# Norms between the branches of a two-layer decoder step: unread matmuls in TensorE's wait, the residual updated by VectorE alone in pairs of tiles, the next norm's squares moved into the following group

## Chip, cores and metric

One Trainium2 chip, and on it one core. The metric is the device time of one execution in microseconds (us), the median over the runs shown. The profile is of one execution, recorded by the hardware profiler.

## What is computed

A step of a hybrid decoder with two layers, for 256 prompt tokens and 32 sample tokens (288 columns in all, D = 2048 features). Each layer is a mixer branch and a feed-forward branch, each between two RMS norms, with a residual `h` that lives through the whole step:

```python
for l in range(DEPTH):                      # DEPTH = 2
    a = _rms(h, norm_mix_pre[l])
    y = mixer(a)                            # even layer: pooling and retention; odd layer: spatial gating and convolution (width 31)
    h = h + _rms(y, norm_mix_post[l])
    f = _rms(h, norm_ffn_pre[l])
    f = square(relu(f @ w_up[l])) @ w_down[l]
    h = h + _rms(f, norm_ffn_post[l])

def _rms(x, g):
    return x * rsqrt(mean(x * x, axis=-1) + EPS) * g
```

All in float32. Where one branch ends and the next begins, the kernel must thus finish a norm of `y`, add it to `h`, and start the norm of `h`. There are four such ends; the change touches the three that lie between branches (the last has code of its own).

## The kernel before

Features lie on the 128 partitions and tokens in the 288 columns, so `h` is 16 tiles `[128, 288]` in one buffer. Weights stream from HBM in pieces of 128x1024 floats. Each piece is split in two so that the faster float32r matmul gives full precision: ScalarE writes the rounded part `whi` (`emit_hi`), VectorE the rest `wlo = raw - whi` (`emit_lo`); activations are split in the same way into `xhi` (ScalarE, `make_hi`) and `xlo` (VectorE, `make_lo`). One piece is called a sub. `emit_mm` issues its 24 matmuls (line 522): two row blocks by four output blocks by three products (hi·hi, lo·hi, hi·lo). Subs are collected in groups of eight (four in the odd layer's output projection), each with 512 outputs in four banks of PSUM; five banks exist, and a bank comes free when its evacuation has read it.

The order on each engine is the order in which `run()` emits. For each sub it emits some `whi` (a ring of three to five subs), one step of a `pre` generator if the group has one, the `wlo`s, the matmuls, and then `bg_step()`, which advances each background generator in `bgs` by one `yield`. A second list, `fills`, holds work that is emitted only while a small meter per engine says there is room; the odd layer's convolution is there: `conv_all` (five of eight channel tiles, 31 taps each on VectorE, the rows `conv<-gx` and `odds<-gx`) and `conv_pool` (three tiles, taps on ScalarE with adds on GpSimd). They start when the first odd group has been evacuated, and `post_o` drains what is left of them behind the first half of the output projection, followed by `conv_out`, the convolution's layer norm.

A boundary is the `pre` generator of the first group of a branch (`boundary`, line 344). `last_rs()` sums the squares of `y` with matmuls of one column (line 273); GpSimd takes the power -0.5 (`sm`); `spread` broadcasts the result over the partitions with six float32 passes (line 252) into a bank `pb`. Then, for each tile k: `grow_h` (VectorE: `tmp = y * pb`), `add_h` (`h += tmp`; VectorE for tiles 0, 1 and the even ones, GpSimd for the odd ones), `make_hi`, the square of `h` on ScalarE with its add into `accs[1]` on GpSimd (`add_sq`), and, one pair later, `make_lo`. The first group uses `xhi` and `xlo` without the pre-norm's factor, as that is a factor per token: its results are copied to `y` tiles (`defer`), and a background generator `rest` runs `finish_pre` (sums the squares, spreads the factor, copies it to `rb`) and then evacuates the group with `rb`. Later groups are evacuated with `rb` directly.

Of the kernel before, what the change touches and what calls it, by code (L numbers as in the profile page):

```python
# [19 lines left out]
T = SEQ + NS  # L20
# [83 lines left out]
class Meter:  # L104
    """an engine, with the work that is emitted on it and, by estimate, not done yet"""

# [27 lines left out]
def build(tc, ctx, I, O, C):  # L134
# [12 lines left out]
    def tmp():  # L147
        return tp.tile([128, T], F32, tag="tmp", name="tmp")
# [10 lines left out]

    # ------------------------------------------------------------ loads  # L160
    xth = [cp.tile([128, 2, D // 2], F32, tag=f"hidhi{i}", name="xth") for i in range(2)]
# [65 lines left out]

    # ------------------------------------------------------------ norms
    P = {}
# [9 lines left out]
    def rs_from(cols, d):  # L239
        """cols: the sums of 128 or fewer tokens each"""  # L240
        sm = next_small()
        for t, c in enumerate(cols):
            V.tensor_scalar(out=sm[:c.shape[0], t:t + c.shape[1]], in0=c, scalar1=1.0 / d, scalar2=EPS, op0=MUL,
                            op1=ADD)
        G.tensor_tensor(out=sm[:, 4:7], in0=sm[:, 0:3], in1=mhalf[:, 0:3], op=ALU.pow)
        return sm[:, 4:7]
# [9 lines left out]
    def sum_open(rep=None):  # L256
        """the tokens' sums over the features of parts to come; with rep the sample's four times over"""
        P["sums"] = [bank(), 0, rep]
# [81 lines left out]
    def y(k):  # L340
        return Y[k // 8][:, k % 8, :]

    # ------------------------------------------------------------ boundaries
    def boundary(layer, which):
        post = (1, 3)[which]
        nxt = (2, layer) if which == 0 else (0, layer + 1)
        rs = last_rs()
        pb = spread(rs)
        new_x()

        def grow_h(k):
            t = tmp()
            V.tensor_tensor(out=t, in0=y(k), in1=pb[:, :T], op=MUL)
            return t

        def add_h(k, t, eng):
            eng.tensor_tensor(out=h[:, k, :], in0=h[:, k, :], in1=t, op=ADD)

        def first(k):
            make_hi(k, gain(nxt[0], nxt[1], k))  # L360
            add_sq(accs[1], k, h[:, k, :])

        def second(k):
            make_lo(k, gain(nxt[0], nxt[1], k))

        for k in (0, 1):
            add_h(k, grow_h(k), V)
            first(k)
        second(0)
        second(1)  # L370
        for a in range(2, KT, 2):
            tb = grow_h(a + 1)
            add_h(a + 1, tb, G)
            ta = grow_h(a)
            if a > 2:
                second(a - 2)
                second(a - 1)
            add_h(a, ta, V)
            first(a)
            first(a + 1)  # L380
            yield
        second(KT - 2)
        second(KT - 1)
        yield
        yield
# [4 lines left out]
    def last_tiles(src, m):  # L390
        """the squares of the last tiles go to the row sums by themselves"""
        if m < OWN:
            add_sq(accs[0], 12 + m, src)
            return
        s = tmp()
        A.activation(out=s, in_=src, func=AF.Square)
        P["own", m] = s
# [7 lines left out]
    def last_rs():  # L405
        sum_part(accs[0])
        for m in range(OWN, 4):
            sum_part(P["own", m])
        return sum_rs(D)

    def finish_pre():
        yield
        ps = var_of(accs[1])
        yield
        rs = rs_from(ps, D)
        yield
        pb = spread(rs)
        A.copy(out=rb, in_=pb[:, :T])
        yield

    # ------------------------------------------------------------ background work
    bgs, fills = [], []
# [16 lines left out]

    # ------------------------------------------------------------ the stream of weights  # L440
    groups = []
# [49 lines left out]
    def feed_hi(to):  # L491
        """the weights' first parts up to sub to, and more weights on their way"""
        while W["split"] <= min(to, len(subs) - 1):
            fetch()
            emit_hi(W["split"])
            W["split"] += 1
# [7 lines left out]
    def some(n):  # L504
        """n subs more, as far as the ring goes beyond the sub at hand"""
        return min(W["split"] + n - 1, W["now"] + RING + W["extra"] - 1)
# [121 lines left out]

    # ------------------------------------------------------------ feed-forward
    def ffn(layer, last):  # L630
# [56 lines left out]

    # ------------------------------------------------------------ even layer
    evo, ne = _cols(C_EVEN)
# [128 lines left out]
    def ret_k(j):  # L818
        """what the two heads' queries and keys give alone"""
        ep, qk = E["pool"], E["qk"]  # L820
# [72 lines left out]
    def piece(R, j, p):  # L893
        """two batches of a head's sample group: their rows' part from the old state, and the new state"""
        hh, b = p // 4, 2 * (p % 4)
# [175 lines left out]

    # ------------------------------------------------------------ odd layer
    odo, no = _cols(C_ODD)
# [93 lines left out]
    def conv_slow(ct):  # L1167
        """one channel tile's taps on the scalar and Pool engines"""
        dw = dwT.rearrange("p (k t) -> p t k", t=8)
        gx, acc = Q["gx"][ct], Q["conv"][:, ct, 0:SEQ]  # L1170
        for k in range(CK):
            while not room(((A, CAPA), (G, CAPG))):
                yield
            w = dw[:, ct, k:k + 1]
            if k == 0:
                A.activation(out=acc, in_=gx[:, 0:SEQ], func=AF.Identity, scale=w, bias=vec("dw_b", ct))
            else:
                t = Q["pool"].tile([128, SEQ], F32, tag="tap", name="tap", bufs=4)
                A.activation(out=t, in_=gx[:, k:k + SEQ], func=AF.Copy, scale=w)
                G.tensor_tensor(out=acc, in0=acc, in1=t, op=ADD)  # L1180
# [69 lines left out]
    def layer_norm(src, n):  # L1250
        """src(k): tiles [128, T], their sum in accs[1]; centres them in place and leaves the factor in Q"""
        yield
# [227 lines left out]

    # ------------------------------------------------------------ first layer's input
    def prologue():
# [45 lines left out]

    # ------------------------------------------------------------ the end
    F = {}  # L1530

    def end_h():
        """the residual turned token-major while the last feed-forward runs"""
        F["h"] = W["pool"].tile([128, 2, D], F32, tag="hT", name="hT", bufs=1)
        F["hs"] = W["pool"].tile([128, 512], F32, tag="hTs", name="hTs", bufs=1)
        for k in range(KT):
            turn_tile(h[:, k, :], F["h"], F["hs"], k, A)
            yield
# [74 lines left out]
```

## Time and profile before

| what | value |
|---|---|
| median of 3 runs | 2537.54 us (2537.18 to 2537.67) |
| span of the profiled execution | 2536.2 us |
| TensorE busy | 2436.1 us (96%) |
| VectorE busy | 1397.9 us (55%) |
| ScalarE busy | 1120.8 us (44%) |
| GpSimd busy | 384.4 us (15%) |
| mean granted TensorE clock | 0.981 |
| the three boundaries, first `y * pb` on VectorE | at 456.0, 1286.0 and 1683.9 us |

The page names no time of the profiled execution other than its span from the first to the last instruction; the runs' median lies 1.3 us above it. In the profile PE is TensorE, DVE VectorE, ACT ScalarE and POOL GpSimd. A helper records most instructions of DVE, ACT and POOL, so that they all carry line 119; they are told apart by the names of their tiles, output first. The granted clock is a share of 2.4 GHz: 1.00 is 2.4 GHz, 0.50 is 1.2 GHz, and a value between is a stretch with some of each.

### The profile page before, as it was taken

The numbers are of one execution on the slowest core, as the hardware profiler recorded it, in microseconds if no ns is written. First come the engines' busy times: TensorE is split into PE (matmuls) and PEld (weight loads), VectorE is DVE, ScalarE is ACT, GpSimd is POOL, SyncE is SP. The second block draws the span as 40 slices with busy tenths as digits, with TensorE's granted clock in tenths as the row PEclk, the third lists the DMA queues.
The fourth block names the chain that finished last, engine by engine and source line by source line (L and its number), as shares of the span: only waits on it lengthen the run. The fifth ranks groups of instructions, "written<-read, shape, count | busy, mean of one in ns | idle before, by whom it ended". The sixth has DMA issues, their size and how long they took to land.

```text
span 2536.2 us, 43599 instructions
## 1 busy us (share of the span) xinstructions
PE 2436.1 (96%) x18060; PEld 2400.4 (95%) x18060; DVE 1397.9 (55%) x1838; ACT 1120.8 (44%) x1648; POOL 384.4 (15%) x440
## 2 busy tenths in 40 slices
PE   7999999899999999999988889789999999999998
PEld 6989999899999999999988889789999999999997
DVE  5555564754354445454478978665434444544454
ACT  4443433553443344344454555555444433433453
POOL 2321121300000000000137764340000000000010
PEclk9999999899999999999999999889999999999999
DMA  6556555455555555555444435336555555555542
GB/s 192 165 172 194 171 176 173 133 167 167 166 167 166 166 166 167 167 166 167 158 136 137 131 117 160 112 112 180 169 157 166 166 167 166 165 167 166 167 158 96
DMA packets 220612, 403.52 MB, mean 159 GB/s; under 512 B 14593, under 2 KB 44077, under 8 KB 220358
## 3 DMA queue, kind: packets, MB, share of 16 engines
q1 hardware_dynamic: 214446, 383.53, 49.4%
q0 software_dynamic: 5440, 16.75, 2.1%
q8 instruction: 141, 2.31, 0.4%
q10 hardware_dynamic: 528, 0.46, 0.1%
q14 instruction: 57, 0.47, 0.1%
HBM read 390.77 MB, written 10.95 MB: 158 GB/s over the span
## 4 chain that ended last, share of the span: by engine, by line
PE 84%; DVE 9%; issue 3%; ACT 2%; POOL 1%; DMA 0%; DVEq 0%; POOLq 0%; ACTq 0%
PE mm L522 80%; DVE wlo L119 3%; DVE conv L119 2%; DVE odds L119 1%; DVE tmp L119 1%; DVE xlo L119 1%; DVE h L119 1%; ACT tmp L119 1%; ACT whi L119 1%; PE ms L904 1%; POOL acc L119 0%; PE ms L908 0%; PE ms L1543 0%; PE ms L273 0%; PE ms L252 0%
## 5 line engine op out<-in xcount | busy, mean ns | idle before, releaser
L119 DVE TENSOR_TENSOR wlo<-raw,whi 128x1024 fp32r<-128x1024 f32 x720 | 893.3, 1246 | 808.7 <-ACT whi L119 808.2
L119 ACT ACTIVATE whi<-raw 128x1024 fp32r<-128x1024 f32 x720 | 759.5, 1059 | 1030.3 <-PE mm L522 982.8
L522 PE MATMUL mm<-xhi,whi 128*128 128x288 f32 x3200 | 954.4, 299 | 32.8 <-DVE tmp L119 27.1
L522 PE MATMUL mm<-xhi,wlo 128*128 128x288 f32 x3200 | 953.0, 299 | 18.9 <-DVE wlo L119 18.8
L522 PE MATMUL mm<-xlo,whi 128*128 128x288 f32 x3200 | 924.8, 298 | 0.0
L522 PE MATMUL mm<-hidhi,whi 128*128 128x288 f32 x2560 | 752.0, 295 | 3.5 <-ACT hidhi L119 3.5
L522 PE MATMUL mm<-hidhi,wlo 128*128 128x288 f32 x2560 | 753.9, 295 | 0.9 <-DVE wlo L119 0.9
L522 PE MATMUL mm<-hidlo,whi 128*128 128x288 f32 x2560 | 742.5, 295 | 0.0
L522 PEld LDWEIGHTS mm<-xhi,whi 128*128 128x128 f32 x3200 | 612.9, 192 | 35.7 <-DVE tmp L119 28.5
L522 PEld LDWEIGHTS mm<-xhi,wlo 128*128 128x128 f32 x3200 | 612.5, 191 | 23.7 <-DVE wlo L119 23.4
L522 PEld LDWEIGHTS mm<-xlo,whi 128*128 128x128 f32 x3200 | 601.4, 191 | 0.0
L522 PEld LDWEIGHTS mm<-hidhi,whi 128*128 128x128 f32 x2560 | 482.2, 188 | 4.1 <-ACT hidhi L119 3.6
L522 PEld LDWEIGHTS mm<-hidhi,wlo 128*128 128x128 f32 x2560 | 482.2, 188 | 1.1 <-DVE wlo L119 1.1
L522 PEld LDWEIGHTS mm<-hidlo,whi 128*128 128x128 f32 x2560 | 477.4, 188 | 0.0
L119 POOL TENSOR_TENSOR acc<-acc,tmp 128x288 f32<-128x288 f32 x107 | 102.7, 960 | 1720.6 <-ACT tmp L119 1715.5
L119 POOL TENSOR_TENSOR conv<-conv,tap 128x256 f32<-128x256 f32 x90 | 89.6, 996 | 57.9 <-ACT tap L119 52.8
L119 DVE SCALAR_TENSOR_TENSOR u<-mm,rb 128x288 f32<-128x288 f32 x120 | 54.9, 457 | 78.8 <-PE mm L522 78.8
L119 DVE TENSOR_TENSOR y<-mm,y 128x288 f32<-128x288 f32 x112 | 51.0, 457 | 84.4 <-PE mm L522 84.4
L119 ACT ACTIVATE xhi<-h,gT 128x288 fp32r<-128x288 f32 x64 | 33.8, 529 | 64.1 <-DVE h L119 64.1
L119 ACT ACTIVATE u<-u 128x288 f32<-128x288 f32 x128 | 55.3, 432 | 10.0 <-DVE u L119 10.0
L119 ACT ACTIVATE hidhi<-u 128x288 fp32r<-128x288 f32 x128 | 56.9, 445 | 4.1
L119 DVE SCALAR_TENSOR_TENSOR conv<-gx,dwT,conv 128x256 f32<-128x256 f32 x75 | 54.5, 726 | 0.0
(237 smaller groups left out, 1090.3 us busy)
## 6 DMA issues: line engine op xcount, KB each, us to landing
raw<-in_w_up SPq DMA_DIRECT2D x256, 512.0 KB, 3.8
raw<-in_w_down SPq DMA_DIRECT2D x256, 512.0 KB, 3.8
raw<-in_w_in_even SPq DMA_DIRECT2D x56, 512.0 KB, 3.7
raw<-in_w_out_even SPq DMA_DIRECT2D x32, 512.0 KB, 4.0
raw<-in_w_in_odd SPq DMA_DIRECT2D x64, 256.0 KB, 3.0
raw<-in_w_in_odd SPq DMA_DIRECT2D x32, 512.0 KB, 3.7
raw<-in_w_out_odd SPq DMA_DIRECT2D x32, 512.0 KB, 4.3
raw<-in_w_in_even SPq DMA_DIRECT2D x48, 256.0 KB, 3.5
```

Source lines behind the costliest of these rows:

```text
L119: return call(*args, **kw)
L522: PE.matmul(ps, lhsT=lhsT[:, k, c], rhs=rhs, start=s == 0 and k == 0 and which == 0, stop=last and k == 1 and which == 2)
L904: PE.matmul(po[gq:gq + 32, 0:256], lhsT=E["qdm"][:, hh, 32 * (b + i):32 * (b + i + 1)], rhs=s[:, i, :], start=False, stop=b >= 4, tile_pos ...
```

## The change

Three things at each of the three boundaries.

1. `keep_warm(n)` issues n float32 matmuls of 128x288 into a bank that nothing reads: two behind the one-column sums, three behind `spread`.
2. The residual is updated by VectorE alone, in place in the `y` tiles, and from tile 2 on two tiles (576 columns) in one instruction; `tmp` buffers and GpSimd are no longer used for it.
3. The squares of `h` and their adds leave the boundary. `finish_pre` issues them, four tiles a step, so they stand in the group behind the boundary's first one, and everything that waits for `rb` (the evacuation of the first group, and what that starts) comes four subs later.

```diff
+    def keep_warm(n):
+        ps = bank()
+        for _ in range(n):
+            PE.matmul(ps[:, :T], lhsT=ones, rhs=accs[0][:, :T], start=True, stop=True)
+
     def boundary(layer, which):
-        post = (1, 3)[which]
         nxt = (2, layer) if which == 0 else (0, layer + 1)
         rs = last_rs()
+        keep_warm(2)
         pb = spread(rs)
+        keep_warm(3)
         new_x()
 
-        def grow_h(k):
-            t = tmp()
-            V.tensor_tensor(out=t, in0=y(k), in1=pb[:, :T], op=MUL)
-            return t
-
-        def add_h(k, t, eng):
-            eng.tensor_tensor(out=h[:, k, :], in0=h[:, k, :], in1=t, op=ADD)
-
-        def first(k):
-            make_hi(k, gain(nxt[0], nxt[1], k))
-            add_sq(accs[1], k, h[:, k, :])
+        def grow(k, n):
+            t = Y[k // 8][:, k % 8:k % 8 + n, :]
+            V.tensor_tensor(out=t, in0=t, in1=pb[:, :T].unsqueeze(1).to_broadcast([128, n, T]), op=MUL)
+            V.tensor_tensor(out=h[:, k:k + n, :], in0=h[:, k:k + n, :], in1=t, op=ADD)
+            for i in range(n):
+                make_hi(k + i, gain(nxt[0], nxt[1], k + i))
 
         def second(k):
             make_lo(k, gain(nxt[0], nxt[1], k))
 
-        for k in (0, 1):
-            add_h(k, grow_h(k), V)
-            first(k)
+        grow(0, 1)
+        grow(1, 1)
         second(0)
         second(1)
         for a in range(2, KT, 2):
-            tb = grow_h(a + 1)
-            add_h(a + 1, tb, G)
-            ta = grow_h(a)
+            grow(a, 2)
             if a > 2:
                 second(a - 2)
                 second(a - 1)
-            add_h(a, ta, V)
-            first(a)
-            first(a + 1)
             yield
...
     def finish_pre():
+        for a in range(0, KT, 4):
+            for k in range(a, a + 4):
+                add_sq(accs[1], k, h[:, k, :])
+            yield
         yield
         ps = var_of(accs[1])
```

How the order moves, at the three places of which the prediction speaks.

VectorE at the first boundary: tiles 6 and 7, the `wlo` of the group's third sub, tiles 8 and 9, the next `wlo`. Before (`ms` is the bank `pb`, `y_3861` and `y_3862` are the two halves of `y`):

```order
L119 TENSOR_TENSOR tmp<-y_3861,ms 128x288 x2
L119 SCALAR_TENSOR_TENSOR xlo<-h,gT,xhi 128x288 x2
L119 TENSOR_TENSOR h<-h,tmp 128x288
L119 TENSOR_TENSOR wlo<-raw,whi 128x1024
L119 TENSOR_TENSOR tmp<-y_3862,ms 128x288 x2
L119 SCALAR_TENSOR_TENSOR xlo<-h,gT,xhi 128x288 x2
L119 TENSOR_TENSOR h<-h,tmp 128x288
L119 TENSOR_TENSOR wlo<-raw,whi 128x1024
```

Now:

```order
L119 TENSOR_TENSOR y_3861<-y_3861,ms 128x576
L119 TENSOR_TENSOR h<-h,y_3861 128x576
L119 SCALAR_TENSOR_TENSOR xlo<-h,gT,xhi 128x288 x2
L119 TENSOR_TENSOR wlo<-raw,whi 128x1024
L119 TENSOR_TENSOR y_3862<-y_3862,ms 128x576
L119 TENSOR_TENSOR h<-h,y_3862 128x576
L119 SCALAR_TENSOR_TENSOR xlo<-h,gT,xhi 128x288 x2
L119 TENSOR_TENSOR wlo<-raw,whi 128x1024
```

Per pair of tiles VectorE has one product and one add of 576 columns where it had two products and one add of 288; the other add was GpSimd's. The `wlo`s keep their places between the pairs.

ScalarE at the end of the first boundary's group. Before:

```order
L119 ACTIVATE xhi<-h,gT 128x288
L119 ACTIVATE tmp<-h 128x288
L119 ACTIVATE whi<-raw 128x1024 x2
L119 COPY y_3861<-mm 128x288 x4
L119 ACTIVATE whi<-raw 128x1024 x6
L119 COPY rb<-ms 128x288
```

Now (`acc_76` is `accs[1]`, `tmp<-h` a square):

```order
L119 COPY y_3861<-mm 128x288 x4
L119 ACTIVATE acc_76<-h 128x288
L119 ACTIVATE tmp<-h 128x288 x3
L119 ACTIVATE whi<-raw 128x1024 x2
L119 ACTIVATE tmp<-h 128x288 x4
L119 ACTIVATE whi<-raw 128x1024 x2
L119 ACTIVATE tmp<-h 128x288 x4
L119 ACTIVATE whi<-raw 128x1024 x2
L119 ACTIVATE tmp<-h 128x288 x4
L119 ACTIVATE whi<-raw 128x1024 x4
L119 COPY rb<-ms 128x288
```

Four squares now stand between the copies of the first group and the `whi` of the next group's second sub, and four more behind each two `whi`.

VectorE in the odd layer, where the first half of the output projection ends and `conv_out` begins (the last `wlo`, the end of the taps, the first instruction of the layer norm). Before:

```order
L119 SCALAR_TENSOR_TENSOR odds<-gx,dwT,odds 128x256
L119 TENSOR_TENSOR wlo<-raw,whi 128x1024
L119 SCALAR_TENSOR_TENSOR conv<-gx,dwT,conv 128x256
L119 TENSOR_TENSOR conv<-conv,odds 128x256
L119 TENSOR_TENSOR wlo<-raw,whi 128x1024
L119 TENSOR_TENSOR conv<-conv,mean 128x288 x8
```

Now, the end of the same stretch; between its `wlo` and the `wlo` ahead of that stand seven taps, and behind it eleven, of which the last six are shown:

```order
L119 SCALAR_TENSOR_TENSOR odds<-gx,dwT,odds 128x256
L119 SCALAR_TENSOR_TENSOR conv<-gx,dwT,conv 128x256
L119 SCALAR_TENSOR_TENSOR odds<-gx,dwT,odds 128x256
L119 SCALAR_TENSOR_TENSOR conv<-gx,dwT,conv 128x256
L119 SCALAR_TENSOR_TENSOR odds<-gx,dwT,odds 128x256
L119 SCALAR_TENSOR_TENSOR conv<-gx,dwT,conv 128x256
L119 TENSOR_TENSOR conv<-conv,odds 128x256
L119 TENSOR_TENSOR conv<-conv,mean 128x288 x8
```

Of the 155 taps one stood behind the last `wlo` but one; now 18 do.

## Rows read from the trace of the kernel before

**Rows 1.** The page, part 1: busy time, share of the span, instructions.

```profile
PE 2436.1 (96%) x18060; PEld 2400.4 (95%) x18060; DVE 1397.9 (55%) x1838; ACT 1120.8 (44%) x1648; POOL 384.4 (15%) x440
```

**Rows 2.** TensorE's waits, whole span: total us, times, longest us.

```profile
PE mm L522 <- DVE tmp L119: 27.1, 6, 9.1
PE mm L522 <- DVE wlo L119: 19.6, 18, 2.8
```

**Rows 3.** Timeline of TensorE, first boundary: start us, us, instruction, [idle before <-releaser].

```profile
450.82 2.13 PE L273 MATMUL ms<-cg,tmp 128*128 128x1 f32 x18
454.41 1.49 PE L252 MATMUL ms<-cg,sm 128*128 128x128 f32 x6 [1.46 <-POOL sm L119]
457.57 0.61 PE L522 MATMUL mm<-xhi,whi 128*128 128x288 f32 x1 [1.67 <-ACT xhi L119]
...
469.11 0.40 PE L522 MATMUL mm<-xhi,wlo 128*128 128x288 f32 x1 [2.07 <-DVE wlo L119]
```

**Rows 4.** Windows of 1 us there: busy PE, PEld, DVE, ACT, POOL, PEclk, DMA, GB/s.

```profile
453.00:454.00 1.00, 0.00 (x0) 0.00 (x0) 0.38 (x3) 0.00 (x0) 0.50 (x1) 0.71 0.35 57
...
457.00:458.00 1.00, 0.43 (x2) 0.43 (x3) 0.97 (x3) 1.00 (x3) 0.00 (x0) 0.50 0.04 8
...
463.00:464.00 1.00, 1.00 (x7) 1.00 (x7) 1.00 (x2) 0.17 (x1) 1.00 (x2) 0.67 0.00 0
```

**Rows 5.** Timeline of VectorE, first boundary.

```profile
456.00 0.46 DVE L119 TENSOR_TENSOR tmp<-y,ms 128x288 f32<-128x288 f32 x1 [2.59 <-PE ms L252]
...
458.85 0.81 DVE L119 TENSOR_TENSOR tmp<-y,ms 128x288 f32<-128x288 f32 x2
...
467.85 1.21 DVE L119 TENSOR_TENSOR wlo<-raw,whi 128x1024 fp32r<-128x1024 f32 x1
468.98 0.81 DVE L119 TENSOR_TENSOR tmp<-y,ms 128x288 f32<-128x288 f32 x2
469.71 1.49 DVE L119 SCALAR_TENSOR_TENSOR xlo<-h,gT,xhi 128x288 fp32r<-128x288 f32 x2
471.12 1.05 DVE L119 TENSOR_TENSOR h<-h,tmp 128x288 f32<-128x288 f32 x1
472.10 1.21 DVE L119 TENSOR_TENSOR wlo<-raw,whi 128x1024 fp32r<-128x1024 f32 x1
```

**Rows 6.** VectorE by form: a product with PSUM, 512 columns: busy us, mean ns.

```profile
L119 DVE TENSOR_TENSOR smk<-ms,ce 128x512 f32<-128x512 f32 x3 | 2.1, 685 | 0.9 <-PE ms L845 0.9
```

**Rows 7.** Timeline of TensorE: one float32 matmul of 128x288, two passes.

```profile
76.22 0.65 PE L779 MATMUL ms<-tmp,wpl 128*128 128x288 f32 x2
```

**Rows 8.** Timeline of ScalarE: end of the first boundary's group; later, three squares.

```profile
492.69 0.40 ACT L119 COPY y<-mm 128x288 f32<-128x288 f32 x1 [0.39 <-PE mm L522]
492.98 3.90 ACT L119 ACTIVATE whi<-raw 128x1024 fp32r<-128x1024 f32 x4
...
1610.13 1.18 ACT L119 ACTIVATE tmp<-conv 128x288 f32<-128x288 f32 x3
```

**Rows 9.** Timeline of GpSimd: adds of squares; the sums ahead of the layer norm.

```profile
481.74 1.93 POOL L119 TENSOR_TENSOR acc<-acc,tmp 128x288 f32<-128x288 f32 x2 [1.36 <-ACT tmp L119]
...
1590.46 6.42 POOL L119 TENSOR_TENSOR acc<-acc,conv 128x288 f32<-128x288 f32 x6
```

**Rows 10.** Timeline of VectorE, odd layer: a deferred evacuation, a tap beside GpSimd, taps alone.

```profile
1337.67 1.19 DVE L119 TENSOR_TENSOR tmp<-y,rb 128x288 f32<-128x288 f32 x3
...
1382.48 1.05 DVE L119 SCALAR_TENSOR_TENSOR conv<-gx,dwT,conv 128x256 f32<-128x256 f32 x1
...
1602.49 0.47 DVE L119 SCALAR_TENSOR_TENSOR conv<-gx,dwT,conv 128x256 f32<-128x256 f32 x1
1602.88 0.47 DVE L119 SCALAR_TENSOR_TENSOR odds<-gx,dwT,odds 128x256 f32<-128x256 f32 x1
```

**Rows 11.** Timeline of TensorE, odd layer: behind the third group, and the drain.

```profile
1389.71 0.61 PE L522 MATMUL mm<-xhi,whi 128*128 128x288 f32 x1 [9.14 <-DVE tmp L119]
...
1607.97 0.75 PE L1255 MATMUL ms<-acc,cg 128*128 128x288 f32 x2 [1.54 <-POOL acc L119]
```

## The prediction, made before the change was run

> **What bounds the kernel now.** The page's first part says that TensorE is busy in 96% of the span [rows 1], so only the remaining 100 us, or work taken from TensorE itself, can be won. The change adds a little TensorE work and moves none of it, so I read which waits stand at the boundaries. In TensorE's waits, those for VectorE's `wlo` sum to 19.6 us and those for its `tmp` to 27.1 us [rows 2]. The timeline of the first boundary shows where they lie: behind the one-column sums TensorE waits 1.46 us for GpSimd's power, runs the six passes of `spread`, waits 1.67 us for the first `xhi`, and later 2.07 us for the third sub's `wlo` [rows 3]. The windows show that the clock has already dropped when `spread` runs: 0.71, then 0.50 in the first sub, and up again at 463 to 464 [rows 4].
>
> The cause of the `wlo` waits is VectorE's own pace. One period of the first group (`wlo`, two products, two `xlo`, one add) runs from 467.85 to 472.10, that is 4.25 us [rows 5]. A mean matmul is 2436.1 us / 18,060 = 0.135 us [rows 1], so 24 of them are 3.2 us: inside this group TensorE is fed more slowly than it could work. VectorE, then, sets the end of that group.
>
> **Residual on VectorE, in pairs.** VectorE takes over GpSimd's add, but pays less per column. One product of 512 columns with PSUM takes 0.685 us [rows 6], so 576 columns are about 0.76, or 0.80 with the step to the add that needs it. Two products of 288 take 0.81 [rows 5]; an add of 576 columns is one instruction for two, so I take 0.66, between 0.5 and 0.81. The adds of 288 that now take 1.05 us and the two `xlo` that take 1.49 are that slow while GpSimd works on `h` beside them: a tap, which like `xlo` has two inputs and a factor, takes 1.05 us beside GpSimd and alone comes every 0.39 us for 256 columns [rows 10]. With GpSimd silent I take 0.42 for each `xlo`. A `wlo` is 1.13 to the next start [rows 5]. So a period is 0.80 + 0.66 + 0.84 + 1.13 = 3.43 us in place of 4.25, still above TensorE's 3.2. The third sub's `wlo` now starts 11.85 us after the first product [rows 5]. The opening two single tiles keep their 2.85 us (456.00 to 458.85); three pairs (1.46 each with their dependence) and four `xlo` of 0.42 follow, 8.9 us in all: 2.9 earlier. Four more periods give 4 x 0.82 = 3.3. The group's end comes 6.2 us earlier at each of three boundaries, bounds 4 (sharing goes on) and 7.
>
> **Unread matmuls.** One float32 matmul of 288 columns is two passes in 0.65 us from first start to last end [rows 7], of which some 0.48 is passes; at the half clock double. Two fit into the 1.46 us wait at full clock and overrun it by up to 0.5 us at half; three take 1.44 or 2.9 us against the 1.67 us wait [rows 3] and can hold back the first sub by up to 1.2. That is covered: sub three waits for VectorE, not for TensorE, and the group ends when VectorE ends. If that cover were gone it would cost the same 1.2 us. I book nothing, with ends of -0.75 and +0.5 at each boundary.
>
> Does the clock stay up? In the rows, TensorE records are busy from 450.82 to 452.95 with one-column matmuls and the clock falls just behind them; it comes back six microseconds after the dense products begin at 457.57 [rows 3, 4]. Being "busy" with thin matmuls did not hold it. I take it that 1.4 us of dense matmuls between two gaps does not reliably do so either. The Trainium skill ("TensorE: Matmul & The Clock Gate", section "What's actually happening") says that the throttled clock is the default and that activity releases it; by that rule dense matmuls in the gap could keep it released, which is a rival below, while the trace shows a fall behind records that count as busy.
>
> **Squares later.** They leave ScalarE's and GpSimd's work in the first group, where they cost TensorE nothing, and enter the next one. Three squares take 1.18 us, so four take 1.57 [rows 8]. The first four now stand between the group's last copy (492.69 before) and the `whi` of the next group's second sub. A `whi` takes 3.90 / 4 = 0.98 [rows 8]: the second sub's `whi` ends 0.4 + 1.6 + 1.0 = 3.0 us behind the copy's start, and its `wlo` 1.2 later. The sub ahead covers 3.2 us, less than that, so I take a stall of 1.2 us at the feed-forward boundaries and 1.5 at the middle one, between 0 (a longer lead of the ring) and 1.6 (the whole batch). The following two batches have two `whi` each between them: per two subs ScalarE has 2 x 0.98 + 1.57 = 3.5 us of work in 6.4, which fits. GpSimd's 15 adds at 1.93 / 2 = 0.96 [rows 9] are 14.4 us, finished some 15.7 us after the group; TensorE reaches the sums (`var_of`) five subs and the stall later, at 17. No wait, but with 1.3 us to spare.
>
> **Sum per feed-forward boundary:** -6.2 + 1.2 = -5.0 us, twice.
>
> **The odd layer.** Here four subs of delay matter, since the convolution starts when the first odd group is evacuated, and that now comes four subs later. By the order, VectorE's taps stand 15 to 17 behind all the way, and at the end 18 instead of one stand behind the last `wlo` but one. Where the taps end, the layer norm starts; TensorE today waits only 1.54 us there, for GpSimd's sums [rows 11]. A tap alone comes every 0.40 us (1602.49 to 1602.88); beside GpSimd it takes 1.05 as a record [rows 10], some 0.96 from one start to the next if it overlaps the next as the lone one does. So 17 more cost between 17 x 0.40 = 6.8 and 17 x 0.96 = 16.3 us. The first seven run in the group with GpSimd's slow taps beside them, the ten behind the last `wlo` mostly alone: 7 x 0.93 + 10 x 0.40 = 10.5, which I take. The slow taps of GpSimd are later by some five as well, but run beside these.
>
> Against it: behind the third odd group TensorE waits 9.14 us, because the evacuation (`tmp`) stands behind taps on VectorE [rows 11]. 14 taps stand there now instead of 20, which is 6 x 0.96 = 5.8 us less; the deferred evacuation of the first group moves in and takes back about 2.7 (three products take 1.19 alone [rows 10], four 1.6, and beside GpSimd up to 2.2 times that, by the tap's 1.05 against 0.47; I take the middle). Relief: 3.0, bounds 0 and 5.8. Sum of the middle boundary and the odd layer: -6.2 + 1.5 - 3.0 + 10.5 = **+2.8 us**.
>
> **Total:** -5.0 - 5.0 + 2.8 = -7.2 us. The profiled execution spans 2536.2 us, which becomes 2529.0; the median of the runs lies 1.3 us above the span, so **2530.3 us**, faster by 0.3%. About 0.2%, 5.1 us, is what a measurement of this kernel can tell from no change.
>
> **Rivals.**
>
> *Cheap drain.* If GpSimd is done before VectorE's last taps, all 17 cost 0.40, that is 3.7 less than booked, and if the third group's relief is the full 5.8, another 2.8 goes: -13.7, **2523.8 us**. For it: at 1602 the taps already run at 0.40 [rows 10]. Against: in the middle of the layer they do not. Chance 0.19.
>
> *Clock held.* If the unread matmuls keep the clock at 1.00, `spread` takes 0.75 instead of 1.49 us [rows 3] at the first and third boundary; the first subs are faster too, but their gain is swallowed by the wait for `wlo`. That gives 1.5 less, **2528.8 us**. Against it speaks the fall behind the one-column matmuls. Chance 0.11. This is the rule of the Trainium skill's page named above.
>
> *Dear drain.* If all 17 taps run beside GpSimd, the drain costs 16.3, or 5.8 more: -1.4, **2536.1 us**, no change that can be told. For it: GpSimd's slow taps slip too, so they may last as long as VectorE's. Chance 0.16.
>
> *The squares choke ScalarE.* There are 12 batches of four squares at the three boundaries, each 1.57 us ahead of `whi`s that TensorE needs. If the ring has no lead to spare, each batch stalls TensorE in full: 18.8 us instead of the 3.9 booked, 14.9 more, so +7.7 and **2545.2 us**: slower. It decides from about 0.9 us a batch on (12 x 0.9 - 3.9 = 6.9 eats the gain), and is past 0.2% from 1.4 us. Against: between batches ScalarE has 6.4 us for 3.5 us of work. Chance 0.12.
>
> That the unread matmuls do not do what they are there for is part of the forecast; that the instructions are in the new places is certain from the order.
>
> **Numbers.** Forecast 0.42, with 2526.5 to 2534 as its own range (the group's end between 5 and 7 us earlier, the drain by some 3 us either way). The range 2522 to 2538 takes in the cheap drain, the held clock, the dear drain and the mild end of the choked ScalarE. Faster by over 0.2% (below 2532.4): all of the cheap drain and the held clock and the forecast but for 0.05 of it, 0.67. Within: the dear drain and that 0.05, 0.21. Slower: 0.12.
>
> **What would show it.** In the profile after, VectorE's period in the first group should be near 3.4 us, the group's last copy of `y` some 30.5 us behind the first product in place of 36.7, and GpSimd should have no add to `h`. The wait behind the third odd group should shrink to about 6 us, and the wait ahead of the layer norm's sums (line 1255) grow from 1.5 to about 12. If `var_of` (line 296) waits for GpSimd, my 1.3 us of spare was wrong. A period of 4 us or more, a stall in each of the next four subs, or a drain outside 6.8 to 16.3 would make the prediction wrong.

## The result and the profile after

The changed kernel took 2557.51 us (median of 4 runs, 2556.91 to 2560.01) against 2537.61 us: the ratio is 1.0076 (95% interval 1.0062 to 1.009), 19.9 us slower. Forecast were 2530.3 us and a range of 2522 to 2538. The profiled execution spans 2556.1 us.

First part 1 of the page after, which answers to [rows 1]:

```profile
PE 2445.4 (96%) x18090; PEld 2404.5 (94%) x18090; DVE 1384.0 (54%) x1817; ACT 1123.2 (44%) x1648; POOL 380.3 (15%) x419
```

The totals say little: TensorE's busy time grew by 9.3 us, of which the unread matmuls can hold a part, the rest of the 19.9 must be waiting. So the next view is TensorE's waits over the whole span, as in [rows 2]:

```profile
PE mm L522 <- DVE tmp L119: 25.6, 4, 8.7
...
PE ms L296 <- POOL acc L119: 19.1, 3, 8.4
...
PE mm L522 <- DVE wlo L119: 14.2, 12, 2.8
...
PE ms L1255 <- POOL acc L119: 11.7, 1, 11.7
```

Before, line 1255 waited 1.54 us [rows 11] and line 296 (the one-column sums of `var_of`) 8.4 us, once, in the odd layer's own norm. That one is still there; two more of 5.3 us each came, one behind each feed-forward boundary. The waits for `wlo` shrank from 19.6 to 14.2.

To place the loss I use four landmarks, GpSimd's powers: of the three boundaries and, third in order, of the odd layer's norm. They stand in GpSimd's timeline of the kernel after:

```profile
453.43 0.86 POOL L119 TENSOR_TENSOR sm<-sm,cg 128x3 f32<-128x3 f32 x1 [3.92 <-DVE sm L119]
...
1287.30 0.86 POOL L119 TENSOR_TENSOR sm<-sm,cg 128x3 f32<-128x3 f32 x1 [3.69 <-DVE sm L119]
...
1636.19 0.88 POOL L119 TENSOR_TENSOR sm<-sm,cg 128x3 f32<-128x3 f32 x1 [1.65 <-DVE sm L119]
...
1698.88 0.86 POOL L119 TENSOR_TENSOR sm<-sm,cg 128x3 f32<-128x3 f32 x1 [3.49 <-DVE sm L119]
```

and in that of the kernel before:

```profile
453.50 0.86 POOL L119 TENSOR_TENSOR sm<-sm,cg 128x3 f32<-128x3 f32 x1 [3.93 <-DVE sm L119]
...
1284.09 0.86 POOL L119 TENSOR_TENSOR sm<-sm,cg 128x3 f32<-128x3 f32 x1 [3.50 <-DVE sm L119]
...
1618.75 0.88 POOL L119 TENSOR_TENSOR sm<-sm,cg 128x3 f32<-128x3 f32 x1 [1.66 <-DVE sm L119]
...
1681.41 0.86 POOL L119 TENSOR_TENSOR sm<-sm,cg 128x3 f32<-128x3 f32 x1 [3.49 <-DVE sm L119]
```

Stretch A, from the first to the second, holds the first boundary; B, from the second to the third, the middle boundary and the odd layer; C, from the fourth to the span's end, the third boundary. What lies between the third and the fourth takes 62.7 to 62.9 us in all kernels here. Before, A, B and C take 830.6, 334.7 and 854.8 us. After, A is longer by 3.3, B by 14.2, C by 2.4: together 19.9.

**The first group became as fast as forecast.** VectorE at the first boundary, one period from `wlo` to `wlo`:

```profile
464.82 1.22 DVE L119 TENSOR_TENSOR wlo<-raw,whi 128x1024 fp32r<-128x1024 f32 x1
465.95 0.75 DVE L119 TENSOR_TENSOR y<-y,ms 128x576 f32<-128x576 f32 x1
466.73 0.76 DVE L119 TENSOR_TENSOR h<-h,y 128x576 f32<-128x576 f32 x1
467.41 0.94 DVE L119 SCALAR_TENSOR_TENSOR xlo<-h,gT,xhi 128x288 fp32r<-128x288 f32 x2
468.27 1.22 DVE L119 TENSOR_TENSOR wlo<-raw,whi 128x1024 fp32r<-128x1024 f32 x1
```

The period is 468.27 - 464.82 = 3.45 us (before 4.25 [rows 5], forecast 3.43). ScalarE's timeline behind it shows the group's last copy and what then follows:

```profile
486.42 0.40 ACT L119 COPY y<-mm 128x288 f32<-128x288 f32 x1 [0.39 <-PE mm L522]
486.72 0.45 ACT L119 ACTIVATE acc<-h 128x288 f32<-128x288 f32 x1
487.06 1.10 ACT L119 ACTIVATE tmp<-h 128x288 f32<-128x288 f32 x3
488.07 1.99 ACT L119 ACTIVATE whi<-raw 128x1024 fp32r<-128x1024 f32 x2
...
494.57 0.45 ACT L119 ACTIVATE tmp<-h 128x288 f32<-128x288 f32 x1 [0.61 <-POOL acc L119]
496.32 0.45 ACT L119 ACTIVATE tmp<-h 128x288 f32<-128x288 f32 x1 [1.30 <-POOL acc L119]
```

The copy starts 30.54 us behind the first product at 455.88 (forecast 30.5, before 36.7 [rows 8]). The 6.2 us were there. The last two rows show where the trouble begins: ScalarE's squares wait for GpSimd, which has not yet used up the `tmp` buffers.

**GpSimd was late.** Its timeline, the fifteen adds together and then six of them singly:

```profile
487.57 20.96 POOL L119 TENSOR_TENSOR acc<-acc,tmp 128x288 f32<-128x288 f32 x15 [33.29 <-ACT tmp L119]
```

```profile
488.46 0.81 POOL L119 TENSOR_TENSOR acc<-acc,tmp 128x288 f32<-128x288 f32 x1
489.34 1.69 POOL L119 TENSOR_TENSOR acc<-acc,tmp 128x288 f32<-128x288 f32 x1
491.11 1.67 POOL L119 TENSOR_TENSOR acc<-acc,tmp 128x288 f32<-128x288 f32 x1
...
496.37 0.81 POOL L119 TENSOR_TENSOR acc<-acc,tmp 128x288 f32<-128x288 f32 x1
...
502.52 0.81 POOL L119 TENSOR_TENSOR acc<-acc,tmp 128x288 f32<-128x288 f32 x1
503.42 1.65 POOL L119 TENSOR_TENSOR acc<-acc,tmp 128x288 f32<-128x288 f32 x1
```

There are two prices here, 0.81 us (six adds) and 1.65 to 1.69 us (nine), and nothing between. VectorE's timeline tells which is which:

```profile
489.14 2.97 DVE L119 TENSOR_TENSOR wlo<-raw,whi 128x1024 fp32r<-128x1024 f32 x2 [6.17 <-ACT whi L119]
492.38 3.24 DVE L119 TENSOR_TENSOR wlo<-raw,whi 128x1024 fp32r<-128x1024 f32 x2 [0.27 <-ACT whi L119]
497.75 3.14 DVE L119 TENSOR_TENSOR wlo<-raw,whi 128x1024 fp32r<-128x1024 f32 x2 [2.13 <-ACT whi L119]
503.02 4.86 DVE L119 TENSOR_TENSOR wlo<-raw,whi 128x1024 fp32r<-128x1024 f32 x3 [2.12 <-ACT whi L119]
```

The adds at 488.46, 496.37 and 502.52 begin while VectorE idles, those at 489.34, 491.11 and 503.42 while a `wlo` runs; with all fifteen it is so. Both lose: two `wlo` take 2.97 and 3.24 us in place of the 2.36 that two take with GpSimd silent. In the mean an add takes 20.96 / 15 = 1.40 us. The Trainium skill ("SBUF — State Buffer", section "Who interferes with whom") has the rule: a VectorE instruction with two inputs in SBUF contends with a GpSimd instruction that reads SBUF, the ports that they share are an exclusive lock, and the order of issue decides which of them is blocked; one with at most a single SBUF input, outside the two-port modes, does not contend. The trace agrees: `wlo` (`raw` and `whi`) has two such inputs. The product with the bank `pb` has one, and in the run with all squares back (below) it takes 0.74 us beside GpSimd's adds where it takes 0.75 here without them, while the two `xlo` take 1.48 in place of 0.94. VectorE's add to `h` has two SBUF inputs as well and takes 0.76 us in both kernels; in that run it is GpSimd that pays there (1.38 us for the add at 475.32). That page spoke against part 3, and I had not weighed it.

**What TensorE paid.** TensorE's timeline, first boundary, at `var_of`:

```profile
502.96 0.29 PE L522 MATMUL mm<-xlo,whi 128*128 128x288 f32 x1
508.59 1.21 PE L296 MATMUL ms<-cg,acc 128*128 128x1 f32 x6 [5.33 <-POOL acc L119]
509.72 0.61 PE L522 MATMUL mm<-xhi,whi 128*128 128x288 f32 x1
```

and the windows of 1 us around it (busy time and count of PE, PEld, DVE, ACT, POOL; PEclk, DMA, GB/s):

```profile
507.00:508.00 1.00, 0.00 (x0) 0.00 (x0) 0.88 (x1) 0.00 (x0) 1.00 (x1) 0.93 0.84 248
508.00:509.00 1.00, 0.41 (x2) 0.42 (x3) 0.00 (x0) 0.00 (x0) 0.53 (x1) 0.50 0.80 215
...
514.00:515.00 1.00, 1.00 (x7) 1.00 (x7) 0.00 (x0) 0.00 (x0) 0.00 (x0) 0.66 0.00 0
515.00:516.00 1.00, 1.00 (x9) 1.00 (x9) 0.00 (x0) 0.58 (x1) 0.00 (x0) 1.00 0.00 0
```

TensorE has nothing to do from 503.3 to 508.6; near the end of that the clock drops to 1.2 GHz, and it stays there until 514.6. From 508.6 on that is 6 us of work at half speed, by estimate 3 us lost on top of the 5.3.

The middle boundary paid in another place. GpSimd's adds, what stands behind them in its queue, and TensorE's transposes of `o`:

```profile
1322.14 19.27 POOL L119 TENSOR_TENSOR acc<-acc,tmp 128x288 f32<-128x288 f32 x15 [33.98 <-ACT tmp L119]
1341.36 1.09 POOL L119 MEMSET o<- 128x1024 f32 x2
...
1343.04 0.66 POOL L119 TENSOR_SCALAR_AFFINE_SELECT o<-o 128x512 f32<-128x512 f32 x1
```

```profile
1343.75 1.12 PE L1132 MATMUL ms<-cg,o 128*128 128x128 f32 x4 [5.09 <-POOL o L119]
```

The mask is a background generator's and has nothing to do with the norm. It stands behind the adds in GpSimd's queue (the MEMSET starts at 1341.36, where the adds end), and TensorE waited for it 5.09 us, with half clock (0.50) behind it until 1350.9. The kernel before had no wait there.

And the drain, at the layer norm of the odd layer:

```profile
1624.84 1.33 PE L1255 MATMUL ms<-acc,cg 128*128 128x288 f32 x2 [11.66 <-POOL acc L119]
```

This is 10.1 us more than the 1.54 before [rows 11]; 10.5 was forecast.

What had been booked against the drain did not come: the wait behind the third odd group, 9.14 us before [rows 11] and forecast to shrink to about 6, is 8.73. TensorE's timeline, and the last but one of the VectorE taps ahead of the evacuation:

```profile
1393.91 0.61 PE L522 MATMUL mm<-xhi,whi 128*128 128x288 f32 x1 [8.73 <-DVE tmp L119]
```

```profile
1392.03 1.05 DVE L119 SCALAR_TENSOR_TENSOR conv<-gx,dwT,conv 128x256 f32<-128x256 f32 x1
```

The last seven taps ahead of the evacuation now take 6.0 us (1387.38 to 1393.41), since GpSimd's convolution work runs beside them until 1392.8; before, that ended at 1386.6, six of the last seven taps ran alone, and the seven took 3.2 us (1385.98 to 1389.22). So the taps that were left there cost more each.

### The profile page after: what moved, and what is told of

Read it like the earlier page. It is cut to its first block, busy times and chain, and to the rows that moved or that the text cites. A ratio compares the mean times of both kernels' runs of the same rounds, so it can differ in the third digit from the quotient of the medians.

```text
span 2556.1 us, 43630 instructions
## 1 busy us (share of the span) xinstructions
PE 2445.4 (96%) x18090; PEld 2404.5 (94%) x18090; DVE 1384.0 (54%) x1817; ACT 1123.2 (44%) x1648; POOL 380.3 (15%) x419
## 4 chain that ended last, share of the span: by engine, by line
PE 84%; DVE 7%; issue 3%; POOL 3%; ACT 2%; DMA 0%; DVEq 0%; POOLq 0%; ACTq 0%
PE mm L522 80%; POOL acc L119 2%; DVE wlo L119 2%; DVE conv L119 2%; DVE odds L119 1%; ACT whi L119 1%; ACT tmp L119 1%; PE ms L904 1%; POOL prod L119 0%; DVE tmp L119 0%; PE ms L908 0%; DVE y L119 0%; PE ms L273 0%; DVE h L119 0%; DVE xlo L119 0%
## 5 line engine op out<-in xcount | busy, mean ns | idle before, releaser
L522 PE MATMUL mm<-xhi,whi 128*128 128x288 f32 x3200 | 951.5, 299 | 25.6 <-DVE tmp L119 25.6
L522 PE MATMUL mm<-xhi,wlo 128*128 128x288 f32 x3200 | 949.7, 298 | 14.2 <-DVE wlo L119 14.2
L119 POOL TENSOR_TENSOR acc<-acc,tmp 128x288 f32<-128x288 f32 x107 | 120.7, 1128 | 1768.9 <-ACT tmp L119 1762.2
```

Of the source, the lines that this page charges most:

```text
L119: return call(*args, **kw)
L522: PE.matmul(ps, lhsT=lhsT[:, k, c], rhs=rhs, start=s == 0 and k == 0 and which == 0, stop=last and k == 1 and which == 2)
```

## Experiments

The theory: **the late sums**. Part 2 gains what was forecast; part 3 loses it again, since GpSimd's adds, slowed by VectorE's `wlo`, end after TensorE has reached `var_of` (or the mask), and since a late `rb` lengthens the drain. Rivals: the squares choke ScalarE, whoever adds them; the unread matmuls or the pairs cost. The kernel before took 2540.2 to 2542.4 us (medians) beside these runs, above the 2537.5 from which the expectations in us were worked out, so I compare ratios to it, and the stretches A, B and C as differences from the profile of before, in us, which leave out the identical code ahead of the first boundary. The two ways differ by a few us, because the change itself was measured beside the faster 2537.6: where a run is compared with the change (e1, e4, e8), I give the difference of the medians too. Line numbers shift by a few between the runs; I use the change's.

| run | ratio (95%) | A | B | C |
|---|---|---|---|---|
| the change | 1.0076 (1.0062 to 1.009) | +3.3 | +14.2 | +2.4 |
| e1_squares_back | 0.9978 (0.9968 to 0.9987) | -1.3 | -0.8 | -2.1 |
| e2_vector_sums | 0.9978 (0.9969 to 0.9988) | -4.8 | +7.0 | -6.5 |
| e3_no_unread | 1.0075 (1.006 to 1.009) | +2.9 | +14.1 | +2.4 |
| e4_sums_read_later | 1.0014 (1.0005 to 1.0024) | -5.3 | +15.1 | -5.1 |
| e5_squares_in_y | 0.9954 (0.9939 to 0.9969) | -4.8 | +0.6 | -5.6 |
| e6_middle_in_place | 0.9945 (0.993 to 0.996) | -5.8 | -0.4 | -5.7 |
| e7_in_y_no_unread | 0.9952 (0.9936 to 0.9969) | -5.7 | +1.1 | -5.8 |
| e8_unread_in_the_wait | 1.0046 (1.0031 to 1.0061) | -0.2 | +13.6 | -0.4 |
| e9_in_y_read_at_once | 0.9946 (0.9933 to 0.996) | -4.7 | -1.3 | -4.6 |

**Part 3 undone** (`finish_pre` as before).

```diff
+                add_sq(accs[1], k + i, h[:, k + i, :])      # in grow(), behind make_hi
...
-        for a in range(0, KT, 4):                            # in finish_pre()
-            for k in range(a, a + 4):
-                add_sq(accs[1], k, h[:, k, :])
-            yield
```

> The changed kernel with part 3 undone: the squares and their GpSimd adds stand in the boundary again, finish_pre as before; the unread matmuls and VectorE's pairs stay. Theory (the late sums): the change lost its time because GpSimd's fifteen adds, 1.40 us each in the next group, end after TensorE has reached the one-column sums of var_of (5.3 us of wait, then some 6.7 us at half clock, worth 3.3), and because the convolution ends 10.7 us later. Without part 3 both go: no wait of line 296 for acc ahead of the feed-forward groups, 1.5 us ahead of line 1255, and the first groups end 4 us earlier than in the kernel before rather than 6.2, as GpSimd's adds of squares slow VectorE again: 2537.6 - 3 x 4 = about 2525.5 us (2520 to 2531). Rival (the pairs or the unread matmuls cost): 2545 us or more.

Measured: ratio 0.9978, some 5.6 us faster than before, and faster than the change by 23 (medians) to 25 us (ratios). No wait of line 296 behind the feed-forward boundaries, 3.1 us ahead of line 1255. So neither the pairs nor the unread matmuls make the kernel slower. The gain was smaller than expected, though (12 us, with 7 as the least), and VectorE's timeline shows why:

```profile
473.36 1.22 DVE L119 TENSOR_TENSOR wlo<-raw,whi 128x1024 fp32r<-128x1024 f32 x1
474.49 0.75 DVE L119 TENSOR_TENSOR y<-y,ms 128x576 f32<-128x576 f32 x1
475.27 0.76 DVE L119 TENSOR_TENSOR h<-h,y 128x576 f32<-128x576 f32 x1
475.95 1.50 DVE L119 SCALAR_TENSOR_TENSOR xlo<-h,gT,xhi 128x288 fp32r<-128x288 f32 x2
477.37 1.83 DVE L119 TENSOR_TENSOR wlo<-raw,whi 128x1024 fp32r<-128x1024 f32 x1
```

With GpSimd's adds of squares back, a period is 4.01 us, not far from 4.25, and the group's last copy stands 35.13 us behind the first product: 1.6 us earlier than before, where the expectation had 4. It is not GpSimd's adds to `h` alone that slow VectorE but its adds of squares beside `xlo` and `wlo` too; pairs alone bring little as long as GpSimd works there.

**The same late squares, summed by VectorE.**

```diff
-                add_sq(accs[1], k, h[:, k, :])
+                add_sq(accs[1], k, h[:, k, :], V)
```

> The changed kernel with the late squares summed by VectorE, which is idle there more than half the time, and no longer by GpSimd. Theory (GpSimd's late sums): the waits of line 296 (5.3 us, twice) and of line 1132 (5.1 us, once) and the half clock behind each (3.3 us) go, the drain ahead of the layer norm (10.7 us) stays: 2557.5 - 3 x 8.5 = about 2532 us (2528 to 2537). Rival (the squares choke ScalarE, whoever adds them): ScalarE's order is the same, so 2553 us or more.

Measured: ratio 0.9978, 5.6 us below the kernel before, as expected (2532 against 2537.5). A and C come out 4.8 and 6.5 us shorter than before, where 5.0 was forecast for the change. ScalarE's order is the same as in the change, so it is not ScalarE's squares that choke. VectorE's and TensorE's timelines at the first boundary:

```profile
491.36 2.14 DVE L119 TENSOR_TENSOR acc<-acc,tmp 128x288 f32<-128x288 f32 x4
493.42 2.35 DVE L119 TENSOR_TENSOR wlo<-raw,whi 128x1024 fp32r<-128x1024 f32 x2
```

```profile
503.04 0.65 PE L296 MATMUL ms<-cg,acc 128*128 128x1 f32 x6
```

Four adds take 2.14 us, two `wlo` 2.35, and TensorE runs `var_of` at 503.04 without a wait; in the change it arrived at 503.3 and waited. B stays 7.0 us longer; the drain is still there (11.7 us of wait at line 1255, as in the change).

**Without the unread matmuls.**

```diff
-        keep_warm(2)
-        keep_warm(3)
```

> The changed kernel without the fifteen unread matmuls. Theory (the late sums): they end the half clock at the boundary some 6 us earlier, but the third sub waits for VectorE's wlo anyway, so 2557 to 2561 us, the first group ending within 1 us of where it ends with them, and the waits of line 296 at 5 us still. Rival (they hold back TensorE at the boundary): 2553 us or less.

Measured: ratio 1.0075, A, B and C within 0.4 us of the change's. The unread matmuls neither cost nor bring anything here in sum. At the middle boundary they did hold VectorE back a little: its first `y * pb` starts 2.61 us behind GpSimd's power in the change, 1.81 without them and 1.87 in the kernel before.

**The sums read three subs later, behind the two feed-forward boundaries.** The group behind the first one is here evacuated before `rb` is written, so with the factor of the norm before: the results are wrong, the instructions are the same, and the run serves for its time alone.

```diff
-        yield
+        P["ends"] = P.get("ends", 0) + 1
+        for _ in range(1 if P["ends"] == 2 else 4):
+            yield
         ps = var_of(accs[1])
```

> The changed kernel with var_of three subs later behind the two feed-forward boundaries; the middle one as it is. Theory (the late sums): GpSimd has 9.6 us more and needs 5.3, so at these two boundaries the wait and the half clock behind it go: 2557.5 - 2 x 8.6 = about 2540 us (2538 to 2545), and in the profile 5 us of wait is left at the middle boundary alone. Rival (the squares choke ScalarE): the stalls of TensorE for wlo behind the boundary stay and grow, 2552 us or more.

Measured: ratio 1.0014, 15.7 us below the change by the ratios and 13.9 by the medians (17 expected). A and C are 8.6 and 7.5 us shorter than in the change and B is not, and 5.1 us of wait is left at line 1132 alone. Nothing was changed but the place at which TensorE reads the sums: the wait for them, and what it drags behind, is the whole loss at the two feed-forward boundaries.

**More unread matmuls, inside the wait.**

```diff
+        P["ends"] = P.get("ends", 0) + 1
+        if P["ends"] != 2:
+            keep_warm(10)
         ps = var_of(accs[1])
```

> The changed kernel with ten more unread matmuls (4.8 us at full clock) ahead of var_of behind the two feed-forward boundaries, inside the 5.3 us in which TensorE waits for GpSimd. Theory (the half clock behind that wait costs 3.3 us each time): the granted clock stays at 1.00 behind the wait and 2 x 3.3 = 6.6 us come back: about 2551 us (2549 to 2553). Rival (the clock falls all the same, or nothing hangs on it): 2556 to 2560 us.

Measured: A is 3.5 us shorter than in the change, C 2.9; ratio 1.0046, 7.6 us below the change by the ratios and 4.6 by the medians (6.6 expected). TensorE's timeline, and one window of it:

```profile
510.02 0.76 PE L296 MATMUL ms<-cg,acc 128*128 128x1 f32 x6 [0.50 <-POOL acc L119]
```

```profile
510.00:511.00 1.00, 0.98 (x8) 0.95 (x9) 0.18 (x3) 0.00 (x0) 0.00 (x0) 1.00 0.92 344
```

The wait is filled and the clock stays at 2.4 GHz behind it (0.50 in the change). So a wait of 5.3 us cost some 3 us more in half clock. That also is the one place where unread matmuls paid.

**Late squares summed by VectorE, but the middle boundary in place.**

```diff
+                if which == 1:                               # in grow(), behind make_hi
+                    P["mid"] = True
+                    add_sq(accs[1], k + i, h[:, k + i, :])
...
+        if not P.pop("mid", False):      # in finish_pre(); set by the middle boundary, whose grow() adds the squares itself
             for a in range(0, KT, 4):
                 for k in range(a, a + 4):
-                    add_sq(accs[1], k, h[:, k, :])
+                    add_sq(accs[1], k, h[:, k, :], V)
                 yield
```

> The late squares summed by VectorE behind the two feed-forward boundaries, and at the middle boundary squares and GpSimd adds inside the boundary, as in the kernel before. Theory (the drain is the price of a late rb in the odd layer): the middle boundary with the odd layer costs what it did in the run with all squares back (0.8 us less than before), the other two what they did in the run with VectorE's sums (5.0 and 6.5 us less): about 12 us below the kernel before, 2525 us (2522 to 2529), with about 3 us of wait ahead of line 1255 in place of 11.7. Rival (the drain is longer because of the pairs or of VectorE's load, not of the late rb): 2532 us or more, the wait at 1255 near 12 us.

Measured: ratio 0.9945, 14 us below the kernel before; 2526.89 us against 2542.4 beside it. Against the run with all late squares on VectorE, B falls from +7.0 to -0.4 and the wait ahead of line 1255 from 11.7 to 3.1. A late `rb` in the odd layer thus costs 7.4 us net.

**Squares in the used-up `y` tiles, summed by VectorE in wide adds.**

```diff
+                if k + i < 4:                                # in grow(), behind make_hi
+                    add_sq(accs[1], k + i, h[:, k + i, :])
+                else:
+                    A.activation(out=y(k + i), in_=h[:, k + i, :], func=AF.Square)
...
-        for a in range(0, KT, 4):                            # in finish_pre()
-            for k in range(a, a + 4):
-                add_sq(accs[1], k, h[:, k, :])
-            yield
+        s = Y[1]
+        V.tensor_tensor(out=s[:, 0:4, :], in0=s[:, 0:4, :], in1=s[:, 4:8, :], op=ADD)
+        V.tensor_tensor(out=s[:, 0:4, :], in0=s[:, 0:4, :], in1=Y[0][:, 4:8, :], op=ADD)
+        yield
+        V.tensor_tensor(out=s[:, 0:2, :], in0=s[:, 0:2, :], in1=s[:, 2:4, :], op=ADD)
+        V.tensor_tensor(out=s[:, 0, :], in0=s[:, 0, :], in1=s[:, 1, :], op=ADD)
+        V.tensor_tensor(out=accs[1][:, :T], in0=accs[1][:, :T], in1=s[:, 0, :], op=ADD)
```

> A version meant to keep the gain of both parts: ScalarE squares h inside the boundary, tile by tile, into the y tiles that the residual has just used up (tiles 0 to 3 by GpSimd's adds as before), and VectorE sums the twelve in five wide adds, 3.9 us in all, in the two subs behind the group; var_of one sub later than in the kernel before, not four. Theory (what costs is the late sums, and for the drain each sub by which rb is late): the first groups end 6.2 us earlier as in the changed kernel, no wait of line 296 behind them, and the drain grows by about a quarter of 10.7: -6 - 6 - 3 = -15 us against the kernel before, about 2523 us (2519 to 2528). Rival (the gain of the pairs is given back behind the group in any case, as ScalarE and VectorE still have the squares to do): within 5 us of the kernel before.

Measured: ratio 0.9954, 11.7 us below the kernel before (15 expected, at least 9.5). The drain is 7.7 us of wait, more than the 4 that a quarter of it would make.

**The same without the unread matmuls** (the cut is against the version just above).

```diff
-        keep_warm(2)
-        keep_warm(3)
```

> The version with the squares in the y tiles, without the unread matmuls. Theory (VectorE sets the end of the first group, not TensorE's clock): the same time within 1.5 us of the one with them. Rival (in the faster boundary the clock counts): 3 to 9 us slower than with them, up to 3 us at each boundary.

Measured: ratio 0.9952, 2529.0 us against 2529.3 with them. The rival, 3 to 9 us slower because the clock counts in the faster boundary, did not come.

**Squares in the `y` tiles, with `var_of` at its old place** (the cut is again against the version with `var_of` one sub later).

```diff
         V.tensor_tensor(out=s[:, 0:4, :], in0=s[:, 0:4, :], in1=Y[0][:, 4:8, :], op=ADD)
-        yield
         V.tensor_tensor(out=s[:, 0:2, :], in0=s[:, 0:2, :], in1=s[:, 2:4, :], op=ADD)
```

> The version with the squares in the y tiles, with all five wide adds of VectorE in the first sub behind the group and var_of where the kernel before has it, so that rb is not late at all. Theory (each sub by which rb comes late lengthens the drain): the wait ahead of line 1255 falls from 7.7 us to about 3, as in the run with the middle boundary in place, and the odd layer gives back some 4 us, less up to 1 us for the wlo behind the adds: about 14 us below the kernel before, a ratio of 0.9945 (0.993 to 0.9955). Rival (the drain that is left has another cause, or var_of waits for VectorE's adds): no faster than with the later var_of, 0.9955 or more.

Measured: ratio 0.9946, as expected. The wait at line 1255 fell from 7.7 to 5.4, not to 3, and the intervals of the two versions overlap: that it is faster than with the later `var_of` isn't shown, and what is left of the drain, with `rb` no longer late by the order, stays open. TensorE now comes to the end of the odd layer earlier while VectorE's taps are as many; that would explain it but wasn't tried.

The version with the middle boundary in place and this last one both beat the kernel before by some 0.55%, and the change by more; which of the two is faster can't be told.

## Why the prediction was wrong

- **Residual in pairs:** right, in mechanism and size. Period 3.45 us (3.43), last copy 30.54 us behind the first product (30.5). Its lower bound was too high: 4 us earlier if the sharing went on, where the run with the squares back found 1.6, with a period of 4.01.
- **Unread matmuls booked at nothing:** right in sum, and for the reason given: without them the time was the same. At the middle boundary they delayed the first product by some 0.7 us, a little more than the 0.5 that I had allowed. The rival of the held clock did not come: the clock fell at 453 to 454 as before (0.62 in that window). It came back earlier, at 456 to 458 in place of 463 to 464 [rows 4], but that was swallowed by the wait for `wlo`.
- **Squares later:** this is the step that failed, in its sentences "GpSimd's 15 adds at 1.93 / 2 = 0.96 [rows 9] are 14.4 us, [...] No wait, but with 1.3 us to spare." Forecast was 14.4 us, measured 20.96. I took the 0.96 from a pair of which one add ran beside a product with the bank (0.81 us) and one beside the short `xlo` (1.04), and moved the adds beside `wlo`s, where one takes 1.67. TensorE came to the sums when I had said, 16.8 us behind the start of the group's last copy (forecast 17); GpSimd was done 22.1 us behind it (forecast 15.7). The spare of 1.3 us became a wait of 5.3, and TensorE's half clock behind it made it more than 8. Against the -5.0 forecast, the two feed-forward boundaries came out 8.3 and 7.4 us dearer (A and C), 15.7 of the 27 us by which the forecast missed. My line on what would show this (line 296 waiting for GpSimd) held.
- **The stall that I did book was too long:** 1.2 us at the second sub, where my own terms made 3.0 + 1.2 - 3.2 = 1.0; it is 0.73 us. At the middle boundary it is 0.42 in place of 1.5.
- **The middle boundary:** the same late adds cost 5.1 us and half clock, through the mask behind them in GpSimd's queue, which I had not followed: a term that I put at nothing. I counted each moved instruction's own time and not what queued behind it.
- **The drain:** right. 10.5 forecast for 17 taps, 10.1 more of wait measured, and in the way forecast: the seven taps ahead of the last `wlo` take 6.0 us (1611.82 to 1617.83, six of them beside GpSimd), the eleven behind it 0.40 each.
- **The relief behind the third odd group:** wrong. 3.0 us booked, 0.4 came (9.14 to 8.73), because the taps left there ran beside GpSimd's convolution work. All waits for `tmp` in the odd layer together fell by 1.5 us.
- **Rivals:** none of mine had this mechanism. The one on the slow side put the trouble on ScalarE; the run with VectorE's sums has ScalarE's order unchanged and no loss at the feed-forward boundaries.

The loss adds up roughly. For the middle boundary with the odd layer: -5.4 (the group's end, counted from GpSimd's power: 6.1 less the 0.7 of the unread matmuls), +0.4 (stall at the second sub), +5.1 and by estimate +3.6 (mask, and 7.2 us at half clock), -1.5 (the waits for `tmp`, 27.1 to 25.6), +1.2 (one wait for a `wlo`, 0.90 to 2.08), +1.5 (waits for `vg`, 0.5 to 2.0), +10.1 (drain): 15.0 for the 14.2 in B. The mask with its half clock, the `wlo` and the `vg` stood in no term of mine.

## What to carry to other kernels

Before work is moved on an engine, price it beside what runs at the new place, not at the old one: an add of GpSimd cost 0.81 us alone and 1.67 beside VectorE's `wlo`. A margin of a microsecond or two at a point where TensorE reads a result is no margin: here a wait of 5 us cost 8, with the half clock behind it. And look at what stands behind the moved instructions in their queue, also when it belongs to something else.

## What was not expected of the hardware

- In the change GpSimd's adds have two sharp prices, 0.81 and 1.65 to 1.69 us, by whether a `wlo` runs when they begin. Beside shorter VectorE instructions, in the run with all squares back, they lie between as well (0.90 to 1.67).
- A wait of 5.3 us let TensorE's clock drop to 1.2 GHz just before it ended (0.93, then 0.50), and 6 us of work were then done at half speed. Ten unread matmuls in the wait kept it at 1.00.
- Where VectorE set the pace, the clock was worth nothing: a half-clock stretch shorter by some 7 us (first boundary) moved the time by less than the measurement can tell.
